# Sums of weight halves interleaved with joins, range sums on ScalarE, and four more units by seven, in a hybrid decoder step

## The chip, the cores and the metric

The kernel runs on one core of a Trainium2 chip. Five engines matter: TensorE (PE, with its weight loads shown as PEld), VectorE (DVE), ScalarE (ACT), GpSimd (POOL) and SyncE (SP), which issues most of the weight transfers. Each engine works through its own list of instructions in order; one waits for another by semaphores. The metric is the device time of one execution in microseconds (us); lower is better.

## The reference

One layer of a decoder, for 256 prompt tokens and 8 sample tokens (T = 264 columns together), model width 2048:

```python
def swiglu(x, wg, wu, wd):
    return (jax.nn.silu(x @ wg) * (x @ wu)) @ wd

h = h + 0.5 * swiglu(rmsnorm(h, norm_ffn1[l]), ffn1_gate[l], ffn1_up[l], ffn1_down[l])
mix, C_f, n_f, m_f, buf = mixing_block(rmsnorm(h, norm_mix[l]), w_in[l], ...)
h = h + mix
h = h + 0.5 * swiglu(rmsnorm(h, norm_ffn2[l]), ffn2_gate[l], ffn2_up[l], ffn2_down[l])
```

The inner width of both feed-forward networks (FFNs) is 5504, that is 43 blocks of 128. The mixing block, a gated linear memory beside a short convolution, takes part in the change only with its output projection. Everything is in float32; the weights are read once.

## The kernel before

**Numbers in halves.** A float32 weight is split into two float16 parts: ScalarE casts the high part (`high`, L257) and VectorE subtracts it from the weight and writes the low part (`low`, L265). Activations are split in the same way. A regular product needs three float16 matmuls for each block of 128 rows: high by high, high by low, low by high (`three`, L397 to L399), each on 264 columns.

**Units.** An FFN is computed in two halves of its 43 blocks (0 to 21, then 22 to 42). For each block there is a gate product and an up product over 16 blocks of rows; this text calls them one unit. After the units of a half come its 16 down products. A regular unit is two products of 48 matmuls.

**By seven.** Some units, and some pairs of down products (20 in the two FFNs, and two pairs of output products in the mixing block), are made together by `product_pair` (L460). It does the high-by-high terms as they are (L486), for two products on 264 columns. The two correction terms are made for two outputs, two neighbouring blocks of rows and two halves of the tokens at once, a product of 2x2 by 2x2 block matrices, by a scheme that needs seven block products instead of eight, each on 132 columns (L469, L470). For this it needs

- sums of the weights' halves: `weight_sums` makes four tiles `s` out of each weight tile in three VectorE steps, L372, L375 and L376, each of which reads the result of the one before;
- sums of token halves of the activations (`token_sums`, L458), once for a group of eight blocks;
- a `join` of the results: ScalarE copies one part out of PSUM (L523), then `rest` runs on VectorE: L526, L527, L530, L531 and L532, and a reduction (L533) that adds up the magnitudes in the last 16 columns of both products, for a verdict on the ranges at the end (`twins`, read by `judge_early`).

A weight tile has up to 16 blocks of 128 by 128. A unit by seven uses two such tiles, each with the first or second eight row blocks of both gate and up; a regular unit uses one tile for the gate and one for up.

**Banks.** PSUM has eight banks, handed out by `bank()`. A regular product takes one, a unit by seven three: `one`, `other` and `more`.

**The order of work** is written by hand. `product` and `product_pair` first call `fetch` until about three weight tiles are on their way (`AHEAD`, `room`): it starts the transfer from the sync queue, issues the cast on ScalarE and keeps the VectorE part of the tile in `held`. `release`, called in the middle of a product and at its end, issues that part: `low`, and for tiles by seven the three steps of `weight_sums` straight behind it. `tick` counts half products in `seq`; `at(delta, fn)` puts a function on an agenda, and the tick that reaches its time runs it. In this way the join of a unit by seven is issued on VectorE in the first tile of the next unit (`at(1.5, rest)`), its SiLU half a product later on ScalarE (`at(2, gate)`), and its product and split later still. Since each engine keeps its order, a step issued late stands behind everything issued earlier on that engine.

**Where units by seven stand.** `GU_SEVEN` lists the blocks, spread evenly over a stretch by `spread(b0, b1, n)`: n of the blocks from b0 to b1 - 1. Before, in the first FFN 9, 11, 12, 14, 16, 17, 19 and 20 in the first half; in the second FFN 5, 7, 8, 10, 11, 13, 14, 16, 17, 19 and 20; in both second halves 24, 25, 27, 28, 30, 31, 33, 34, 36, 37, 39, 40 and 41.

The functions in question, with the line numbers of the profile:

Of the kernel before, what the change touches and what calls it, by code (L numbers as in the profile page):

```python
# [8 lines left out]
F32 = mybir.dt.float32  # L9
# [3 lines left out]
AF = mybir.ActivationFunctionType  # L13
ALU = mybir.AluOpType

D = 2048
KB = D // 128
SEQ = 256
NS = 8
T = SEQ + NS  # L20
DFF = 5504
NFB = DFF // 128
# [15 lines left out]
SEEN = 16  # L38
# [13 lines left out]
def spread(b0, b1, n):  # L52
    return [b0 + i for i in range(b1 - b0) if (i + 1) * n // (b1 - b0) > i * n // (b1 - b0)]


GU_SEVEN = {
    "1": spread(8, 21, 8) + spread(23, NFB - 1, 13), "2": spread(4, 21, 11) + spread(23, NFB - 1, 13),
}
DOWN_SEVEN = {
    ("1", 0): (1, 2, 3, 5, 6, 7), ("1", 1): (1, 2, 4, 5),  # L60
# [5 lines left out]
TH = T // 2  # L66
# [114 lines left out]
def step(ctx: ExitStack, tc: tile.TileContext, a: dict, shared, bad=None):  # L181
    nc = tc.nc
# [14 lines left out]
    tmp = ctx.enter_context(tc.tile_pool(name="tmp", bufs=2))  # L197
# [73 lines left out]
    def fetch():  # L271
# [46 lines left out]
        if not lag[0]:  # L318
            release()
# [14 lines left out]
    def take(key):  # L334
        got, hi, lo, n, _ = ready.pop(0)
        assert got == key, (got, key)
        return hi, lo, n

    def release():
        for lows, tile_, parts in held:  # L340
            for x in lows:
                low(*x)
            ready.append(tile_)
            if tile_[0][1] in ("gu", "dd"):
                sums.append(weight_sums(parts, tile_[3]))
        held.clear()

# [18 lines left out]
    def weight_sums(w, n):  # L366

        m = n // 2
        s = spool[0].tile([128, 4, WK // 2, 2, 128], PART, tag="s", name="s", bufs=3)[:, :, :m]
        a_, b_, d_ = (w[:, i : i + 2 * m - 1 : 2] for i in (0, 1, n + 1))  # L370
        bc = w[:, 1 : 2 * n - 1].rearrange("p (g k) h m -> p g k h m", g=2)[:, :, 0 : 2 * m - 1 : 2]
        nc.vector.tensor_tensor(  # L372
            s[:, 0:2], bc, d_.unsqueeze(1).to_broadcast([128, 2, m, 2, 128]), op=ALU.add
        )
        nc.vector.tensor_tensor(s[:, 2], s[:, 1], b_, op=ALU.add)  # L375
        nc.vector.tensor_tensor(s[:, 3], s[:, 2], a_, op=ALU.add)  # L376
        return s


    seq, agenda = [0], {}  # L380

    def at(delta, fn, *args):
        agenda.setdefault(int(seq[0]) + delta, []).append((fn, args))

    def tick(step=None):
        if step is None:
            seq[0] = int(seq[0]) + 1
        else:
            seq[0] += step
        for fn, args in agenda.pop(seq[0], []):  # L390
            fn(*args)

    def bank():
        return psum.tile([128, 512], F32, tag="ps", name="ps", bufs=8)
# [65 lines left out]
    def product_pair(key, x, forms, order):  # L460


        one, other, more = bank(), bank(), bank()
        left, right = slice(0, TH), slice(TH, T)
        spare = slice(T, T + TH)
        count, k0 = len(order), 0

        def correct(ps, w, x, first, last):
            nc.tensor.matmul(ps, w[0], x[:, 1], start=first, stop=False)  # L469
            nc.tensor.matmul(ps, w[1], x[:, 0], start=False, stop=last)  # L470

        while k0 < count:
            while room() or not ready:
                fetch()
            hi, lo, n = take(key)
            if room():
                fetch()
            if k0 in (0, WK):
                tick()
            s = sums.pop(0)  # L480
            (hi0, lo0), (hi1, lo1) = ((hi[:, r:], lo[:, r:]) for r in (0, n))
            xs = [x[order[k0 + i]] for i in range(n)]
            last = k0 + n == count
            for ps, hi, lo in ((one, hi0, lo0), (other, hi1, lo1)):
                for i in range(n):
                    nc.tensor.matmul(  # L486
                        ps[:, :T], hi[:, i], xs[i][:, 0], start=(k0 + i == 0), stop=False
                    )
                if n % 2:
                    correct(ps[:, :T], (hi[:, n - 1], lo[:, n - 1]), xs[n - 1], False, False)  # L490
            release()
            if last or k0 == 0:
                tick(0.5)
            for f in range(7):
                for i in range(n // 2):
                    first = k0 + i == 0
                    end = last and i == n // 2 - 1 and f in (2, 5, 6)
                    e, o = 2 * i, 2 * i + 1
                    t = forms[k0 // 2 + i]
                    a_, b_, c_ = (hi0[:, e], lo0[:, e]), (hi0[:, o], lo0[:, o]), (hi1[:, e], lo1[:, e])  # L500
                    w = (a_, b_, c_, *((s[:, f, i, 0], s[:, f, i, 1]) for f in (1, 0, 2, 3)))[f]
                    ps, rhs, own = (
                        (one[:, left], xs[e][:, :, left], False),
                        (one[:, spare], xs[o][:, :, left], False),
                        (other[:, left], t[:, 3], False),
                        (more[:, TH : 2 * TH], t[:, 0], True),
                        (more[:, 2 * TH : 3 * TH], t[:, 1], False),
                        (more[:, left], t[:, 2], False),
                        (one[:, right], xs[e][:, :, right], False),
                    )[f]  # L510
                    correct(ps, w, rhs, first and own, end)
            k0 += n
        return one, other, more

    def join(banks):


        one, other, more = banks
        y = spool[0].tile([128, 4, TH], F32, tag="y4", name="y4", bufs=2)
        u = t264("ta")[:, :TH]  # L520
        p = more[:, : 3 * TH].rearrange("p (n t) -> p n t", n=3)
        z = y[:, 0:4].rearrange("p (g s) t -> p g (s t)", g=2)
        nc.scalar.copy(y[:, 0], one[:, T : T + TH])  # L523

        def rest():
            nc.vector.tensor_tensor(u, y[:, 0], p[:, 0], op=ALU.subtract)  # L526
            nc.vector.tensor_tensor(  # L527
                y[:, 1:3], p[:, 1:3], u.unsqueeze(1).to_broadcast([128, 2, TH]), op=ALU.add
            )
            nc.vector.tensor_tensor(y[:, 3], p[:, 1], y[:, 2], op=ALU.add)  # L530
            nc.vector.tensor_tensor(z[:, 0], one[:, :T], z[:, 0], op=ALU.add)  # L531
            nc.vector.tensor_tensor(z[:, 1], other[:, :T], z[:, 1], op=ALU.subtract)  # L532
            nc.vector.tensor_reduce(  # L533
                twins[:, :, next(twin)], y[:, 1:4:2, TH - SEEN :],
                axis=mybir.AxisListType.X, op=ALU.add, apply_absolute_value=True,
            )

        return z, rest

# [112 lines left out]
    if half_size:  # L652
# [3 lines left out]
        twins = const.tile([128, 2, PAIRS], F32, name="twins")  # L656
        twin = iter(range(PAIRS))
# [547 lines left out]
        return ps, 128.0 * (len(verdicts) + n) - 0.5  # L1205

    if half_size:
        at(2 * NFB + 2 * KB - 2, judge_early)
    ffn("2", n2, done, end=end)
    cols = spans[-1]  # L1210
    scaled(0, 4, cols, nc.sync)
# [751 lines left out]
```

## Time and profile before

| what | us |
|---|---|
| median of three runs | 1785.66 (1784.39 to 1786.18) |
| profiled execution | 1784.75, its span 1783.0 |
| TensorE busy in the span | 1769.2 |
| VectorE busy | 1628.6 |
| ScalarE busy | 881.4 |
| GpSimd busy | 180.1 |

The span runs from the first to the last instruction of the program; what lies around it (1.75 us here) is in the time, not in the rows. The rows of a profile give an instruction's line, engine, operation, what it writes and reads by the program's own names, the shape, how often it occurs, and how long it takes; the idle time of the engine ahead of it stands in brackets or in the last column, with what ended it. TensorE's matmuls are pipelined: a row's duration is longer than the distance to the next row's start, and the distance is what a matmul takes out of the time. The granted clock of TensorE was 0.998 over the span.

### The profile page before, as it was taken

What the parts mean: (1) busy time and instruction counts of PE and PEld (TensorE: products, weight loads), DVE (VectorE), ACT (ScalarE), POOL (GpSimd) and SP (SyncE); (2) the same over time, 40 slices, a digit from 0 to 9 for tenths busy, and PEclk for the clock granted to TensorE, in tenths of its full rate; (3) what the DMA queues carried; (4) which work ended last, traced back from release to release, by engine and by line L of the source; (5) the groups of instructions that cost most, each with busy time, mean ns of one, the idle gap of its engine ahead of it and who ended that gap; (6) DMA issues with size and microseconds to landing.
All of it is one profiled execution on the core that took longest, in us unless ns stands there. A gap on an engine that the chain in (4) does not pass through costs nothing.

```text
span 1783.0 us, 45308 instructions
## 1 busy us (share of the span) xinstructions
PE 1769.2 (99%) x19802; PEld 1599.4 (90%) x19802; DVE 1628.6 (91%) x2278; ACT 881.4 (49%) x1256; POOL 180.1 (10%) x200
## 2 busy tenths in 40 slices
PE   9999999999999999999999999999999999999997
PEld 8899999999999998888888888899999999999996
DVE  8999989999999998888888798999989999999896
ACT  7644444344444435567566644544444444443443
POOL 0000000000000341212121044000000000000142
PEclk9999999999999999999999999999999999999999
DMA  9656565675655656987787646565655766564653
GB/s 325 220 194 212 180 206 197 205 250 195 213 191 180 203 168 199 305 298 265 281 282 242 222 170 243 184 236 181 216 170 178 236 231 222 184 216 161 202 190 112
DMA packets 102494, 381.51 MB, mean 214 GB/s; under 512 B 10988, under 2 KB 20812, under 8 KB 93328
## 3 DMA queue, kind: packets, MB, share of 16 engines
q1 hardware_dynamic: 93088, 350.52, 58.5%
q0 software_dynamic: 8256, 27.57, 4.5%
q8 instruction: 157, 2.57, 0.6%
q10 hardware_dynamic: 944, 0.45, 0.1%
q14 instruction: 49, 0.40, 0.1%
HBM read 366.72 MB, written 11.78 MB: 212 GB/s over the span
## 4 chain that ended last, share of the span: by engine, by line
PE 96%; DVE 3%; issue 0%; DMA 0%; ACT 0%; DVEq 0%; SPq 0%; ACTq 0%
PE ps L397 18%; PE ps L399 18%; PE ps L398 18%; PE ps L486 14%; PE ps L469 13%; PE ps L470 13%; PE ps L633 1%; DVE w L265 1%; DVE s L372 0%; PE ps L779 0%; PE ps L1596 0%; PE ps L1539 0%; PE ps L1494 0%; DVE s L375 0%; DVE s L376 0%
## 5 line engine op out<-in xcount | busy, mean ns | idle before, releaser
L265 DVE SCALAR_TENSOR_TENSOR w<-wraw,w 128x2048 f16<-128x2048 f32 (+5 forms) x426 | 761.7, 1804 | 56.7 <-ACT w L257 56.0
L257 ACT ACTIVATE w<-wraw 128x2048 f16<-128x2048 f32 (+5 forms) x426 | 633.3, 1503 | 141.6 <-PE ps L470 49.7
L398 PEld LDWEIGHTS <-w 128*128 128x128 f16 x2890 | 282.8, 98 | 42.6
L397 PEld LDWEIGHTS <-w 128*128 128x128 f16 x2890 | 283.0, 98 | 41.2 <-issue 0.4
L399 PEld LDWEIGHTS <-w 128*128 128x128 f16 x2890 | 282.8, 98 | 41.4 <-DVE w L265 0.2
L397 PE MATMUL ps<-r,w 128*128 128x264 f16 x992 | 273.8, 276 | 0.0
L398 PE MATMUL ps<-r,w 128*128 128x264 f16 x992 | 273.8, 276 | 0.0
L399 PE MATMUL ps<-r,w 128*128 128x264 f16 x992 | 273.8, 276 | 0.0
L486 PEld LDWEIGHTS <-w 128*128 128x128 f16 x2368 | 226.9, 98 | 31.2
L397 PE MATMUL ps<-xm,w 128*128 128x264 f16 x896 | 247.3, 276 | 0.0
L399 PE MATMUL ps<-xm,w 128*128 128x264 f16 x896 | 247.3, 276 | 0.0
L398 PE MATMUL ps<-xm,w 128*128 128x264 f16 x896 | 247.3, 276 | 0.0
L470 PEld LDWEIGHTS <-s 128*128 128x128 f16 x2352 | 228.3, 97 | 0.0
L469 PEld LDWEIGHTS <-s 128*128 128x128 f16 x2352 | 226.8, 96 | 1.2 <-DVE y L530 1.2
L372 DVE TENSOR_TENSOR s<-w 128x2048 f16<-128x2048 f16 (+2 forms) x154 | 184.3, 1196 | 9.9 <-DVE w L265 0.5
L486 PE MATMUL ps<-r,w 128*128 128x264 f16 x1440 | 176.7, 276 | 0.0
L470 PEld LDWEIGHTS <-w 128*128 128x128 f16 x1780 | 173.6, 98 | 2.5
L469 PEld LDWEIGHTS <-w 128*128 128x128 f16 x1780 | 173.4, 97 | 2.5
L397 PE MATMUL ps<-a,w 128*128 128x264 f16 (+2 forms) x554 | 144.3, 268 | 0.0
L398 PE MATMUL ps<-a,w 128*128 128x264 f16 (+2 forms) x554 | 144.3, 268 | 0.0
L399 PE MATMUL ps<-a,w 128*128 128x264 f16 (+2 forms) x554 | 144.3, 268 | 0.0
L469 PE MATMUL ps<-f,s 128*128 128x132 f16 x1080 | 133.7, 220 | 0.8 <-DVE y L530 0.8
(305 smaller groups left out, 2832.5 us busy)
## 6 DMA issues: line engine op xcount, KB each, us to landing
wraw<-in_w2gu SPq DMA_DIRECT2D x86, 1024.0 KB, 5.1
wraw<-in_w1gu SPq DMA_DIRECT2D x74, 1024.0 KB, 5.2
wraw<-in_win SPq DMA_DIRECT2D x112, 512.0 KB, 5.2
wraw<-in_w1d SPq DMA_DIRECT2D x20, 1024.0 KB, 5.0
wraw<-in_w2d SPq DMA_DIRECT2D x20, 1024.0 KB, 5.0
wraw<-in_wout SPq DMA_DIRECT2D x24, 512.0 KB, 4.6
wraw<-in_w1d SPq DMA_DIRECT2D x16, 704.0 KB, 4.0
wraw<-in_w2d SPq DMA_DIRECT2D x16, 704.0 KB, 4.1
```

Of the source, the lines that this page charges most:

```text
L257: nc.scalar.activation(dst, src, AF.Copy, scale=scale)
L265: nc.vector.scalar_tensor_tensor(dst, src, scale, hi, op0=ALU.mult, op1=ALU.subtract)
L372: nc.vector.tensor_tensor(s[:, 0:2], bc, d_.unsqueeze(1).to_broadcast([128, 2, m, 2, 128]), op=ALU.add)
L397: nc.tensor.matmul(ps, wh, xk[:, 0, :], start=first, stop=False)
L398: nc.tensor.matmul(ps, wh, xk[:, 1, :], start=False, stop=False)
L399: nc.tensor.matmul(ps, wl, xk[:, 0, :], start=False, stop=last)
L469: nc.tensor.matmul(ps, w[0], x[:, 1], start=first, stop=False)
L470: nc.tensor.matmul(ps, w[1], x[:, 0], start=False, stop=last)
L486: nc.tensor.matmul(ps[:, :T], hi[:, i], xs[i][:, 0], start=(k0 + i == 0), stop=False)
L633: nc.tensor.matmul(ps[j0 + j], w[:, nk * j + k, :], x[k0 + k][:, part, :], start=(k0 + k + n == 0), stop=(k0 + k == KB - 1 and n == 2),)
```

## The change

There are three parts.

*Order of the sums.* `weight_sums` no longer issues its three steps. It puts them on a list, `chain`, and `drain(n)` issues the first n of the list. `drain` is called by `release` ahead of new sums, at the end of each `tick`, in `product_pair` just before a tile's sums are used, and between the steps of `rest`, one at a time.

*The joins.* The last two steps of `rest` change places (the one on `other` now comes first). The reduction on VectorE is gone; in its place `seen` runs on ScalarE, at the next half or whole tick: two ACTIVATE instructions with an accumulated output, one for each of the two products. `judge_early`, which reads these sums, is issued half a product later.

*The blocks.* One more unit by seven in each half of each FFN: 71 pairs in all instead of 67. By `spread`, the first FFN has 9, 10, 12, 13, 15, 16, 18, 19 and 20 in its first half; the second 5, 6, 8, 9, 11, 12, 13, 15, 16, 18, 19 and 20; both second halves 24, 25, 27, 28, 29, 31, 32, 33, 35, 36, 37, 39, 40 and 41.

```diff
 GU_SEVEN = {
-    "1": spread(8, 21, 8) + spread(23, NFB - 1, 13), "2": spread(4, 21, 11) + spread(23, NFB - 1, 13),
+    "1": spread(8, 21, 9) + spread(23, NFB - 1, 14), "2": spread(4, 21, 12) + spread(23, NFB - 1, 14),
 }
...
+    chain = []
+
+    def drain(n=3):
+
+        for step in chain[:n]:
+            step()
+        del chain[:n]
+
     def release():
...
             if tile_[0][1] in ("gu", "dd"):
+                drain()
                 sums.append(weight_sums(parts, tile_[3]))
...
-        nc.vector.tensor_tensor(
-            s[:, 0:2], bc, d_.unsqueeze(1).to_broadcast([128, 2, m, 2, 128]), op=ALU.add
-        )
-        nc.vector.tensor_tensor(s[:, 2], s[:, 1], b_, op=ALU.add)
-        nc.vector.tensor_tensor(s[:, 3], s[:, 2], a_, op=ALU.add)
+        add = nc.vector.tensor_tensor
+        d2 = d_.unsqueeze(1).to_broadcast([128, 2, m, 2, 128])
+        chain.extend((
+            lambda: add(s[:, 0:2], bc, d2, op=ALU.add),
+            lambda: add(s[:, 2], s[:, 1], b_, op=ALU.add),
+            lambda: add(s[:, 3], s[:, 2], a_, op=ALU.add),
+        ))
...
         for fn, args in agenda.pop(seq[0], []):
             fn(*args)
+        drain()
...
                 tick()
+            drain()
             s = sums.pop(0)
...
             nc.vector.tensor_tensor(u, y[:, 0], p[:, 0], op=ALU.subtract)
+            drain(1)
             nc.vector.tensor_tensor(
                 y[:, 1:3], p[:, 1:3], u.unsqueeze(1).to_broadcast([128, 2, TH]), op=ALU.add
             )
+            drain(1)
             nc.vector.tensor_tensor(y[:, 3], p[:, 1], y[:, 2], op=ALU.add)
+            drain(1)
+            at(1 if seq[0] % 1 else 0.5, seen, next(twin))
+            nc.vector.tensor_tensor(z[:, 1], other[:, :T], z[:, 1], op=ALU.subtract)
             nc.vector.tensor_tensor(z[:, 0], one[:, :T], z[:, 0], op=ALU.add)
-            nc.vector.tensor_tensor(z[:, 1], other[:, :T], z[:, 1], op=ALU.subtract)
-            nc.vector.tensor_reduce(
-                twins[:, :, next(twin)], y[:, 1:4:2, TH - SEEN :],
-                axis=mybir.AxisListType.X, op=ALU.add, apply_absolute_value=True,
-            )
+
+        def seen(n):
+            for g in range(2):
+                nc.scalar.activation(
+                    tmp.tile([128, SEEN], F32, tag="seen", name="seen", bufs=2),
+                    y[:, 1 + 2 * g, TH - SEEN :], AF.Abs, accum_out=twins[:, g, n : n + 1],
+                )
...
-        at(2 * NFB + 2 * KB - 2, judge_early)
+        at(2 * NFB + 2 * KB - 1.5, judge_early)
```

## The prediction

> **What bounds the kernel now.** I read the profile page first, then the busy time by stretch, then the order of time on VectorE and TensorE where two stretches end.
>
> ```profile
> span 1783.0 us, 45308 instructions
> ...
> PE 1769.2 (99%) x19802; PEld 1599.4 (90%) x19802; DVE 1628.6 (91%) x2278; ACT 881.4 (49%) x1256; POOL 180.1 (10%) x200
> ```
>
> TensorE is busy 99% of the span, VectorE 91%, ScalarE 49%. Two engines stand near the limit, so the stretches matter more than the page. The next rows are stretches (length, then busy time and count of TensorE, weight load, VectorE, ScalarE and GpSimd, then clock and DMA): one regular gate/up unit, one unit by seven, a group of two by seven and one regular, then the gate/up part of the second half of the first FFN, and the first down projection.
>
> ```profile
> 1607.01:1617.81 10.80, 10.80 (x99) 9.40 (x97) 10.53 (x15) 5.28 (x8) 0.00 (x0) 1.00 0.62 197
> 1617.81:1627.85 10.04, 10.04 (x146) 9.57 (x144) 9.77 (x12) 4.64 (x6) 0.00 (x0) 1.00 0.53 183
> 1576.13:1607.01 30.88, 30.88 (x387) 28.54 (x385) 30.16 (x38) 14.33 (x18) 0.00 (x0) 1.00 0.63 213
> ...
> 372.90:558.18 185.28, 184.70 (x2354) 171.40 (x2352) 178.60 (x222) 82.72 (x103) 0.00 (x0) 1.00 0.57 194
> 253.40:351.31 97.91, 97.91 (x1325) 92.08 (x1323) 93.14 (x109) 39.35 (x34) 0.00 (x0) 1.00 0.60 200
> ```
>
> The reader is to see three things. TensorE has no idle time in a unit: 10.80 us regular, 10.04 us by seven, at a granted clock of 1.00. So TensorE sets the end, and what a unit by seven is worth is 10.80 - 10.04 = 0.76 us. VectorE runs beside it at 30.16 of 30.88 us in a group: it is nearly a second bound. And the gate/up stretch has 185.28 us against 184.70 busy, so almost nothing stalls.
>
> Where it does stall is at the third of three units by seven in a row (blocks 39, 40, 41), once in each FFN. The first fence shows the second of the two places on TensorE, the second what that join line (L530) ends for others.
>
> ```profile
> 1641.02 0.22 PE L470 MATMUL ps<-f,w 128*128 128x132 f16 x1
> 1641.49 0.23 PE L469 MATMUL ps<-f,s 128*128 128x132 f16 x1 [0.26 <-DVE y L530]
> ```
>
> ```profile
>   PEld L469: 1.2, 2
> ```
>
> These matmuls follow each other every 0.06 us, so the start at 1641.49 instead of 1641.08 is a stall of 0.41 us; the two places together cost 1.2 us. The matmul is the first into the third unit's bank `more`. A unit takes three of eight banks, so the third in a row gets one that the first's join still reads, and L530 is the last reader of that join's `more`. Block 39 ended at 1627.85 (above), so a join is late if L530 ends more than 1641.08 - 1627.85 = 13.2 us after its unit.
>
> **What the change costs, part by part.** (1) Four more units by seven, one in each half of each FFN: on TensorE 4 x 0.76 = 3.04 us less. Weight bytes and their DMA issues stay as they are, two 1 MB loads a unit in both forms.
>
> (2) VectorE. This is the whole of its work for one unit by seven, from block 37's and 38's tiles in order of time:
>
> ```profile
> 1609.35 2.29 DVE L265 SCALAR_TENSOR_TENSOR w<-wraw,w 128x2048 f16<-128x2048 f32 x1
> 1611.67 1.23 DVE L372 TENSOR_TENSOR s<-w 128x2048 f16<-128x2048 f16 x1
> 1612.93 0.69 DVE L375 TENSOR_TENSOR s<-s,w 128x1024 f16<-128x1024 f16 x1
> 1613.66 0.69 DVE L376 TENSOR_TENSOR s<-s,w 128x1024 f16<-128x1024 f16 x1
> 1614.27 0.28 DVE L526 TENSOR_TENSOR ta<-y,ps 128x132 f32<-128x132 f32 x1
> 1614.58 0.43 DVE L527 TENSOR_TENSOR y<-ps,ta 128x264 f32<-128x264 f32 x1
> 1615.05 0.29 DVE L530 TENSOR_TENSOR y<-ps,y 128x132 f32<-128x132 f32 x1
> 1615.26 0.42 DVE L531 TENSOR_TENSOR y<-ps,y 128x264 f32<-128x264 f32 x1
> 1615.60 0.42 DVE L532 TENSOR_TENSOR y<-ps,y 128x264 f32<-128x264 f32 x1
> 1616.06 0.19 DVE L533 TENSOR_REDUCE twins<-y 128x2 f32<-128x32 f32 x1
> 1616.17 2.29 DVE L265 SCALAR_TENSOR_TENSOR w<-wraw,w 128x2048 f16<-128x2048 f32 x1
> 1618.49 1.23 DVE L372 TENSOR_TENSOR s<-w 128x2048 f16<-128x2048 f16 x1
> 1619.75 0.69 DVE L375 TENSOR_TENSOR s<-s,w 128x1024 f16<-128x1024 f16 x1
> 1620.48 0.69 DVE L376 TENSOR_TENSOR s<-s,w 128x1024 f16<-128x1024 f16 x1
> 1621.09 0.43 DVE L265 SCALAR_TENSOR_TENSOR a<-y,a 128x264 f16<-128x264 f32 x1
> 1621.43 0.42 DVE L939 SCALAR_TENSOR_TENSOR y<-y,tb 128x264 f32<-128x264 f32 x1
> 1621.78 0.42 DVE L939 SCALAR_TENSOR_TENSOR tc<-ps,tb 128x264 f32<-128x264 f32 x1
> 1622.12 2.28 DVE L265 SCALAR_TENSOR_TENSOR w<-wraw,w 128x2048 f16<-128x2048 f32 x1
> ```
>
> Read it by starts. First tile with the join: 1609.35 to 1616.17, 6.82 us. Second tile: to 1621.09, 4.92. Split of an activation 0.34, product with the gate 0.35. Together 12.43 us against 10.04 on TensorE, so each unit by seven puts VectorE 2.4 us behind. A regular unit has two weight splits of 2.29 - 0.08 = 2.21, one split of 0.34 and one product of 0.34: 5.10 us against 10.80.
>
> Now the gaps. L372 ends at 1612.90 and L375, which reads its result, starts at 1612.93: 0.03 us idle. L376 ends at 1614.35, but L526, which has nothing of it, starts at 1614.27: 0.08 us overlap. All pairs in the fence fall so: a step that needs the one just before it starts 0.03 to 0.04 us after its end, any other 0.08 before. Putting a foreign step between two linked ones is thus worth 0.115 us. The change does that to six links of the first tile (weight split to sum, sum to sum twice, L526 to L527, L527 to L530, and the last join step to the reduction): 0.69 us. The reduction itself leaves, 0.11 us. In the second tile the product comes between the weight split and the first sum, 0.115 us, while the three sums stay linked. A unit falls to 12.43 - 0.69 - 0.11 - 0.115 = 11.52 us.
>
> [...]
>
> The sums of tokens for a group of eight activations come on top, four steps of 0.70 us, 0.35 us a unit:
>
> ```profile
> L458 DVE TENSOR_TENSOR g<-a 128x1056 f16<-128x1056 f16 x16 | 10.6, 702 | 0.1
> ```
>
> Before, two by seven and one regular: 2 x 12.43 + 5.10 + 3 x 0.35 = 31.0 us of VectorE in 30.88 of TensorE. After, three and one, which is the new pattern of the second halves: 3 x 11.52 + 5.10 + 4 x 0.35 = 41.1 us in 40.92. The balance stays what it was, and a run of three costs a backlog of 3 x 1.48 = 4.4 us where two cost 4.8 and the one run of three cost 7.2.
>
> (3) Late joins. There are now eleven runs of three instead of two. In a steady group block 37, which ended at 1607.01, had its L530 end at 1615.34: 8.3 us later against the limit of 13.2, so 4.9 us in hand. In the changed order that step stands before the last sum instead of behind all three, about 1 us earlier behind its weight split. With the smaller backlog I take no stall at any run of three and both old ones gone: -1.2 us. Bounds: none gone (0), or each of nine new runs late by the mean of the two old ones, 0.6 us (+5.2).
>
> (4) ScalarE gets two range sums for each of 71 pairs. The nearest row is its range sum over a regular product, which takes two instructions:
>
> ```profile
> 1582.02 0.18 ACT L670 ACTIVATE seen<-ps 128x16 f32<-128x16 f32 x1
> 1582.08 0.20 ACT L670 ACTIVATION_READ_ACCUMULATOR seen<-ps 128x1 f32 x1
> 1582.17 1.91 ACT L257 ACTIVATE w<-wraw 128x2048 f16<-128x2048 f32 x1
> ```
>
> That is 0.15 us, so 0.30 us a unit on an engine that works 4.64 of 10.04 us there: nothing, covered by its idle time. It adds a wait, though: ScalarE does not go on to the next weight cast until the join's last step is done. In gate/up units the SiLU in front of it waits for that same join already. In down units the wait is new; VectorE then still has the next weight split and its sums, whose cast was issued ahead of the wait, so it does not run dry. I take 0; the other bound is the fourth rival.
>
> (5) The order of the sums. They now follow up to three join steps (0.20 + 0.35 + 0.21 us by starts), so the first sum comes 0.1 us and the last about 0.5 us later behind its weight split, which the shorter queue ahead of it gives back. The verdict on the range sums, 5.3 us of VectorE near the end, moves by half a product and changes places with one weight split; what follows both has the same sum ahead of it. I take 0, at worst one such split of 1.5 us:
>
> ```profile
> 1749.02 0.24 DVE L731 TENSOR_SCALAR ta<-stat 128x172 f32<-128x172 f32 x1
> ...
> 1754.33 3.01 DVE L265 SCALAR_TENSOR_TENSOR w<-wraw,w 128x1408 f16<-128x1408 f32 x2
> ```
>
> Sum: -3.04 - 1.2 = -4.2 us. The profiled execution took 1784.75 us (its span and 1.75 around it), so 1780.5 by its own time. The three runs' median, 1785.66, lies 0.9 above it, so **1781.5 us** as a median.
>
> **Rivals.**
> - The stalls stay. The two waits of 1.2 us remain because blocks 39 to 41 are the same blocks with the same token sums in front. Then only 3.04 us go: 1782.6, or -0.17%. For it: those 2.8 us of token sums fall into that run still. Against: by then VectorE has saved 14 x 0.91 us and paid 11.52 - 5.10 for the added unit, so it comes there some 6 us less loaded.
> - New waits for banks. Each of nine new runs of three pays 0.6 us: 1785.66 - 3.04 + 5.2 = 1787.8. For it: the only run of three in the trace is the only place that stalls. It decides when L530 ends more than 13.2 us after its unit; against it stands the 8.3.
> - Interleaving gains nothing on VectorE, the slower case. Place: second halves, three by seven to one regular. A unit then costs 12.32 us, a group 3 x 12.32 + 6.50 = 43.5 in 40.92, 2.5 us short; 19 blocks are 4.75 groups, 12 us, of which the 4.9 in hand take a part: 7 us in each FFN, 1785.66 - 3.04 + 14 = 1797. It decides once a unit by seven costs VectorE more than (40.92 - 6.50) / 3 = 11.5 us over a whole half plus what is in hand, about 11.8. Against it: the gaps above.
> - ScalarE holds the casts back in the down projections. If each of the 20 down units loses a cast and a range sum (1.91 + 0.30 us) on VectorE, the six of the first take 13.3 us, of which 97.91 - 93.14 = 4.8 idle and 6 x 0.8 of saved links cover 9.6; 3.7 is left, times 20 / 6 for all of them 12 us: 1793.5. It decides only if VectorE has less than 2.2 us of work between the join's end and the next split that needs that cast; the fence shows a split and three sums there, 4.9 us.
>
> **How the numbers follow.** Forecast 0.50, stalls stay 0.24, new waits 0.10, no gain from interleaving 0.06, ScalarE 0.06, others 0.04. A measurement of this kernel can tell about 0.2%, 3.6 us, from no change, and the forecast of 4.2 lies just beyond: of its 0.50 I give 0.40 to faster and 0.10 to same; of the first rival 0.03 and 0.21. With the second mostly same, and the third and fourth slower: faster 0.45, same 0.42, slower 0.13. The range goes from 1780.2 (the forecast less the runs' spread) to 1787.0, which takes in the first rival and part of the second; the likeliest alone would be 1780.5 to 1782.5.
>
> **What would show it.** TensorE busy down by 3 us and no wait of a weight load on a join; stretches of three and one of 40.9 us with VectorE busy for some 40; start to start between L372's and L375's counterparts near 1.14 us in the tile with a join and still 1.26 in the other; ScalarE up by about 20 us. The forecast is wrong if any wait of TensorE on VectorE over 1 us in sum appears in the gate/up stretches or the down projections, or if the links do not shorten.

## The result, and the profile after

The changed kernel takes 1780.43 us in the median of 11 runs (1780.1 to 1781.63), the kernel before, run beside it, 1785.07 (1784.3 to 1786.18): a ratio of 0.9975, with a 95% interval of 0.9967 to 0.9984. That is 4.64 us less. The profiled execution took 1780.68 us with a span of 1779.0, 4.0 us less than before.

The profile page of the changed kernel: busy times, and the first line of the chain of work that ended last (each engine's share of the span).

```profile
PE 1765.9 (99%) x19994; PEld 1600.2 (90%) x19994; DVE 1629.8 (92%) x2255; ACT 906.3 (51%) x1528; POOL 169.2 (10%) x200
...
PE 99%; DMA 0%; DVE 0%; SPq 0%; ACT 0%; issue 0%; DVEq 0%; ACTq 0%
```

The same line of the chain in the kernel before:

```profile
PE 96%; DVE 3%; issue 0%; DMA 0%; ACT 0%; DVEq 0%; SPq 0%; ACTq 0%
```

TensorE is busy 3.3 us less, and VectorE's 3% are gone from the chain: in the feed-forward networks its work no longer holds TensorE back, apart from two matmuls that start 0.08 us late (below). VectorE is as busy as before, with four more units by seven. ScalarE has 24.9 us more.

What TensorE waited for (line, releaser and its line: us in total, times, longest). First the one line of the kernel before that has no counterpart after; then all lines after, which stood before too, the one on a cast (`part`) with 0.5 instead of 0.9 us:

```profile
PE ps L469 <- DVE y L530: 0.8, 2, 0.6
```

```profile
PE ps L1224 <- DVE ta L1218: 2.3, 1, 2.3
PE idle L228 <- DVE ones L218: 1.1, 1, 1.1
PE ps L653 <- ACT part L257: 0.9, 3, 0.5
PE ps L799 <- DVE sq L1186: 0.2, 1, 0.2
```

The wait for the last reader of `more` (L530 before, L545 after) is gone; what remains stands outside the feed-forward networks. (New lines: the sums are L384 to L386, the steps of the join L539, L541, L545, L548, L549, ScalarE's copy L536, the corrections L481 and L482.)

The end of the second FFN's second half, after: the first, third and last of four groups of three units by seven and a regular one, and one unit by seven (length, then busy time and count of TensorE, weight load, VectorE, ScalarE and GpSimd, clock, DMA).

```profile
1480.83:1521.75 40.92, 40.92 (x532) 38.11 (x529) 39.25 (x50) 20.00 (x35) 0.00 (x0) 1.00 0.62 206
...
1562.67:1603.59 40.92, 40.92 (x532) 38.11 (x529) 40.07 (x50) 20.12 (x38) 0.00 (x0) 1.00 0.64 209
1603.59:1644.60 41.01, 41.01 (x531) 38.10 (x529) 40.50 (x53) 18.09 (x35) 0.00 (x0) 1.00 0.51 170
1614.39:1624.43 10.04, 10.04 (x147) 9.57 (x144) 9.80 (x11) 5.25 (x11) 0.00 (x0) 1.00 0.48 147
```

The groups take 40.92 us, exactly 3 x 10.04 + 10.80. VectorE's busy time in the groups shown rises from 39.25 to 40.50, since it has less idle time, and the last group is 0.09 us too long. The place on TensorE:

```profile
1637.59 0.22 PE L482 MATMUL ps<-f,w 128*128 128x132 f16 x1
1637.73 0.23 PE L481 MATMUL ps<-f,s 128*128 128x132 f16 x1
```

0.06 us after 1637.59 would be 1637.65, so this start is 0.08 us late (in the first FFN as much). The unit whose bank it wants, block 39, ended at 1624.43 (fence above), so the bank was wanted 13.2 us after it. The join that frees it is the second L545 in VectorE's rows; the first is the same join of the run before (block 35, which ended at 1562.67 + 10.80 + 10.04 = 1583.51):

```profile
1594.11 0.28 DVE L545 TENSOR_TENSOR y<-ps,y 128x132 f32<-128x132 f32 x1
...
1630.30 1.32 DVE L470 TENSOR_TENSOR g<-a 128x1056 f16<-128x1056 f16 x2
1631.54 0.70 DVE L470 TENSOR_TENSOR g<-g,a 128x1056 f16<-128x1056 f16 x1
...
1637.38 0.29 DVE L545 TENSOR_TENSOR y<-ps,y 128x132 f32<-128x132 f32 x1
```

Block 35's bank is free 1594.39 - 1583.51 = 10.9 us after its unit, block 39's 1637.67 - 1624.43 = 13.24. The changed kernel stands exactly at the limit of 13.2 us, not well inside it. VectorE does not lose this time bit by bit: the first joins of the four runs of three end 8.5, 11.1, 10.9 and 13.2 us after their units, and the two steps up are where the sums of tokens stand (L470, four steps, 1630.30 to the next weight split at 1632.90, 2.6 us). A group without them gains 0.2 us.

VectorE's order of time, the interleaved tile first, then a join that has no sums to mix with:

```profile
1567.39 2.29 DVE L265 SCALAR_TENSOR_TENSOR w<-wraw,w 128x2048 f16<-128x2048 f32 x1
1569.59 0.28 DVE L539 TENSOR_TENSOR ta<-y,ps 128x132 f32<-128x132 f32 x1
1569.79 1.22 DVE L384 TENSOR_TENSOR s<-w 128x2048 f16<-128x2048 f16 x1
1570.93 0.42 DVE L541 TENSOR_TENSOR y<-ps,ta 128x264 f32<-128x264 f32 x1
1571.27 0.68 DVE L385 TENSOR_TENSOR s<-s,w 128x1024 f16<-128x1024 f16 x1
1571.87 0.29 DVE L545 TENSOR_TENSOR y<-ps,y 128x132 f32<-128x132 f32 x1
1572.07 0.68 DVE L386 TENSOR_TENSOR s<-s,w 128x1024 f16<-128x1024 f16 x1
...
1573.36 2.28 DVE L265 SCALAR_TENSOR_TENSOR w<-wraw,w 128x2048 f16<-128x2048 f32 x1
...
1600.79 0.29 DVE L539 TENSOR_TENSOR ta<-y,ps 128x132 f32<-128x132 f32 x1
1601.11 0.43 DVE L541 TENSOR_TENSOR y<-ps,ta 128x264 f32<-128x264 f32 x1
1601.58 0.29 DVE L545 TENSOR_TENSOR y<-ps,y 128x132 f32<-128x132 f32 x1
1601.91 0.43 DVE L548 TENSOR_TENSOR y<-ps,y 128x264 f32<-128x264 f32 x1
```

In the first tile every step starts 0.08 us before its predecessor ends; the tile takes 1573.36 - 1567.39 = 5.97 us, where 6.02 was predicted. In the second piece the steps stand 0.03 to 0.04 us apart, as before the change, and the new order has linked L548 to L545 too. How often each occurs is in VectorE's groups (busy, mean ns of one, idle time just before them):

```profile
L385 DVE TENSOR_TENSOR s<-s,w 128x1024 f16<-128x1024 f16 (+1 forms) x162 | 111.2, 686 | 4.5
...
L541 DVE TENSOR_TENSOR y<-ps,ta 128x264 f32<-128x264 f32 x71 | 30.5, 429 | 1.4
```

The same groups before:

```profile
L375 DVE TENSOR_TENSOR s<-s,w 128x1024 f16<-128x1024 f16 (+2 forms) x154 | 106.7, 693 | 5.3
...
L527 DVE TENSOR_TENSOR y<-ps,ta 128x264 f32<-128x264 f32 x67 | 28.9, 432 | 2.3
```

Before, each of 67 joins had the gap: 2.3 / 67 = 0.034 us. After, 1.4 us are 41 such gaps among 71 joins. So only 30 joins are interleaved; in the other 41 the tile that the join follows belongs to a regular product, or has no sums waiting. In order of time, the join at 1569.59 is of a run's third unit (block 33, which ended at 1562.67), the one at 1600.79 of a second (block 36). Tiles are split ahead of their use: while block 37 is computed, VectorE splits those of the regular block 38, which need no sums. In each of the eight runs of three in the second halves the second unit's join is linked in this way, at the half's end also the last unit's (block 41).

### The profile page after: what moved, and what is told of

Same layout as the page of the kernel before. It is cut to its first block, busy times and chain, and to the rows that moved or that the text cites. A ratio compares the mean times of both kernels' runs of the same rounds, so it can differ in the third digit from the quotient of the medians.

```text
span 1779.0 us, 46011 instructions
## 1 busy us (share of the span) xinstructions
PE 1765.9 (99%) x19994; PEld 1600.2 (90%) x19994; DVE 1629.8 (92%) x2255; ACT 906.3 (51%) x1528; POOL 169.2 (10%) x200
## 4 chain that ended last, share of the span: by engine, by line
PE 99%; DMA 0%; DVE 0%; SPq 0%; ACT 0%; issue 0%; DVEq 0%; ACTq 0%
PE ps L409 17%; PE ps L410 17%; PE ps L411 17%; PE ps L499 16%; PE ps L481 14%; PE ps L482 14%; PE ps L653 1%; PE ps L799 0%; PE ps L1616 0%; DMA raw<-in_w1gu 0%; PE ps L1559 0%; PE ps L1514 0%; DVE h L1167 0%; PE ps L1538 0%; PE ps L1600 0%; PE ps L1537 0%
## 5 line engine op out<-in xcount | busy, mean ns | idle before, releaser
L482 PEld LDWEIGHTS <-s 128*128 128x128 f16 x2480 | 240.7, 97 | 0.0
L481 PEld LDWEIGHTS <-s 128*128 128x128 f16 x2480 | 238.9, 96 | 0.2
L409 PE MATMUL ps<-r,w 128*128 128x264 f16 x864 | 238.5, 276 | 0.0
L410 PE MATMUL ps<-r,w 128*128 128x264 f16 x864 | 238.5, 276 | 0.0
L411 PE MATMUL ps<-r,w 128*128 128x264 f16 x864 | 238.5, 276 | 0.0
L384 DVE TENSOR_TENSOR s<-w 128x2048 f16<-128x2048 f16 (+1 forms) x162 | 191.9, 1185 | 6.1 <-PE ps L482 1.0
L499 PE MATMUL ps<-r,w 128*128 128x264 f16 x1568 | 192.5, 276 | 0.0
L482 PEld LDWEIGHTS <-w 128*128 128x128 f16 x1876 | 183.0, 98 | 2.6
L481 PEld LDWEIGHTS <-w 128*128 128x128 f16 x1876 | 182.8, 97 | 2.6
L481 PE MATMUL ps<-f,s 128*128 128x132 f16 x1176 | 145.6, 220 | 0.0
L482 PE MATMUL ps<-f,s 128*128 128x132 f16 x1176 | 145.4, 219 | 0.0
L409 PE MATMUL ps<-a,w 128*128 128x264 f16 (+2 forms) x554 | 144.3, 268 | 0.0
L410 PE MATMUL ps<-a,w 128*128 128x264 f16 (+2 forms) x554 | 144.3, 268 | 0.0
```

Of the source, the lines that this page charges most:

```text
L384: lambda: add(s[:, 0:2], bc, d2, op=ALU.add),
L409: nc.tensor.matmul(ps, wh, xk[:, 0, :], start=first, stop=False)
L410: nc.tensor.matmul(ps, wh, xk[:, 1, :], start=False, stop=False)
L411: nc.tensor.matmul(ps, wl, xk[:, 0, :], start=False, stop=last)
L499: nc.tensor.matmul(ps[:, :T], hi[:, i], xs[i][:, 0], start=(k0 + i == 0), stop=False)
```

## Experiments

Each ran beside the kernel before on the same chip; the ratios are to that kernel, with 95% intervals. Its medians there were 1784.77 to 1784.83 us, 1785.07 beside the changed kernel, so differences of a few tenths between experiments mean nothing.

**The blocks alone.** The order of VectorE stays as it was.

```diff
@@ GU_SEVEN, kernel before @@
-    "1": spread(8, 21, 8) + spread(23, NFB - 1, 13), "2": spread(4, 21, 11) + spread(23, NFB - 1, 13),
+    "1": spread(8, 21, 9) + spread(23, NFB - 1, 14), "2": spread(4, 21, 12) + spread(23, NFB - 1, 14),
```

> Kernel before with the new blocks alone: 14 units by seven in each second half, 9 and 12 in the first halves; sums and reduction as before. Theory A (VectorE's backlog makes joins late once a unit by seven costs it 12.4 us): a second half of 19 blocks is 14 x 12.43 + 5 x 5.10 + 19 x 0.35 = 206 us of VectorE in 194.6 of TensorE, 12 us short, where before it was 198.8 in 195.3, 3.5 short with 0.6 of stall. So about 9 us of stall in each second half and 0 to 3 in the second FFN's first half: 1785.1 - 3.0 + 19 = about 1801, at least 1793; the trace shows TensorE waiting for joins in the runs of three. Rival B (the units alone carry the gain, the order is immaterial): 1785.1 - 3.0 = 1782 or, if the old stalls go by the new places, 1781.

Measured: 1821.86 us, 1.0209 [1.0195, 1.0223]. The units alone make the kernel 37 us slower: theory A's way, but 21 us more than its 1801. The largest wait of TensorE, then the last of its nine stalls, on VectorE and on TensorE:

```profile
PE ps L469 <- DVE y L530: 32.0, 9, 6.0
```

```profile
1671.28 2.29 DVE L265 SCALAR_TENSOR_TENSOR w<-wraw,w 128x2048 f16<-128x2048 f32 x1
1673.67 1.23 DVE L372 TENSOR_TENSOR s<-w 128x2048 f16<-128x2048 f16 x1
...
1676.27 0.29 DVE L526 TENSOR_TENSOR ta<-y,ps 128x132 f32<-128x132 f32 x1
...
1677.06 0.29 DVE L530 TENSOR_TENSOR y<-ps,y 128x132 f32<-128x132 f32 x1
```

```profile
1671.18 0.22 PE L470 MATMUL ps<-f,w 128*128 128x132 f16 x1
1677.41 0.29 PE L469 MATMUL ps<-f,s 128*128 128x132 f16 x1 [6.01 <-DVE y L530]
```

TensorE wants the bank at 1671.24, and the join that has to free it is still behind a weight split and three sums on VectorE. The account: 3.04 us less for the units, 0.8 less for the two old waits, 32.0 for the nine new ones, together 28.2; the span grew by 37.1. The remaining 8.9 us are in matmuls after the stalls: behind five of them the granted clock is 0.50 for 3.03, 3.58, 4.08, 3.29 and 3.83 us (last section), 17.8 us in all, of which half is lost. (Counted by the starts of matmuls a stall is some 0.15 us longer than by these waits, so the account is good to about 1 us.)

**The order alone.** The changed kernel with the old blocks.

```diff
@@ GU_SEVEN @@
-    "1": spread(8, 21, 9) + spread(23, NFB - 1, 14), "2": spread(4, 21, 12) + spread(23, NFB - 1, 14),
+    "1": spread(8, 21, 8) + spread(23, NFB - 1, 13), "2": spread(4, 21, 11) + spread(23, NFB - 1, 13),
```

> Changed kernel with the old blocks (13, 8, 11): interleaved sums and ScalarE's range sums without more units. Theory A: only the two stalls of 1.2 us go, since TensorE waits for nothing else: 1785.1 - 1.2 = 1783.9, TensorE's waits on joins gone. Rival B: the order does nothing for the stalls, 1785.1. If VectorE were itself on the path all along, more would come off: under 1783.

Measured: 1784.02 us, 0.9998 [0.9989, 1.0007], a span 1.3 us shorter, and no wait of TensorE on a join. By the medians alone this can't be told from no change; in the trace the two old stalls are gone. The order's worth is that it carries four more units.

**The sums in one piece.** The changed kernel, but the three sums are issued as soon as their tile is split, ahead of the join. The move to ScalarE stays.

```diff
@@ weight_sums @@
             lambda: add(s[:, 3], s[:, 2], a_, op=ALU.add),
         ))
+        drain()
```

> Changed kernel, new blocks and ScalarE's range sums, but the three sums are issued straight behind their weight split, so nothing is interleaved. Theory A (a linked step costs 0.115 us more): a unit costs VectorE about 12.3 us instead of 11.5 to 12.0, so second halves are some 10 us short instead of 3.5 before: 6 to 7 us of stall in each, 1785.1 - 3.0 + 14 = about 1796, at least 1787. Rival C (a link costs nothing, the room came from the reduction that moved to ScalarE): as the changed kernel, 1780 to 1782.

Measured: 1822.34 us, 1.0212 [1.0198, 1.0226], the same as the blocks alone. So the move of the range sums does not carry the gain, and the order of sums and joins is worth 42 us, far more than the 16 that theory A gave. That the two kernels take the same is in part chance: TensorE waits 27.6 us for joins here and 32.0 there, but runs 26.4 us at half the clock here and 17.8 there. TensorE's largest wait, and the waits of VectorE and ScalarE in the gate/up part of the first FFN's second half (372 to 556 us):

```profile
PE ps L482 <- DVE y L546: 27.6, 9, 5.1
```

```profile
ACT y L537 <- DVE a L265: 13.3, 3, 4.5
...
DVE w L265 <- ACT w L257: 7.6, 8, 1.9
```

VectorE, which is too slow here, idles 7.6 us in that stretch for a cast of ScalarE. One such place, first on VectorE, then on ScalarE:

```profile
436.75 0.43 DVE L265 SCALAR_TENSOR_TENSOR a<-y,a 128x264 f16<-128x264 f32 x1
437.09 0.43 DVE L960 SCALAR_TENSOR_TENSOR y<-y,tb 128x264 f32<-128x264 f32 x1
439.39 2.29 DVE L265 SCALAR_TENSOR_TENSOR w<-wraw,w 128x2048 f16<-128x2048 f32 x1 [1.88 <-ACT w L257]
```

```profile
437.28 0.27 ACT L537 COPY y<-ps 128x132 f32<-128x132 f32 x1 [4.45 <-DVE a L265]
437.45 1.91 ACT L257 ACTIVATE w<-wraw 128x2048 f16<-128x2048 f32 x1
```

ScalarE's copy writes one of two `y4` tiles, and must wait until VectorE has split the activation out of the tile (436.75). The cast stands behind the copy in ScalarE's queue, and VectorE's next weight split stands behind the cast. A late VectorE thus makes itself later by 1.88 us. Whether this is a real part of the cost is tested further down.

**The reduction on VectorE.** The changed kernel without the move to ScalarE.

```diff
@@ rest @@
-            at(1 if seq[0] % 1 else 0.5, seen, next(twin))
             nc.vector.tensor_tensor(z[:, 1], other[:, :T], z[:, 1], op=ALU.subtract)
             nc.vector.tensor_tensor(z[:, 0], one[:, :T], z[:, 0], op=ALU.add)
+            nc.vector.tensor_reduce(
+                twins[:, :, next(twin)], y[:, 1:4:2, TH - SEEN :],
+                axis=mybir.AxisListType.X, op=ALU.add, apply_absolute_value=True,
+            )
```

> Changed kernel with the range sums back on VectorE, as one reduction at the end of the join, behind the step that it reads. Theory A: 0.11 + 0.115 us a unit more on VectorE, 14 x 0.22 = 3.1 us in a second half whose reserve at the last run of three is used up in the changed kernel: 2 to 3 us of stall in each, 1780.4 + 5 = 1785, between 1782.5 and 1787. Rival (the reduction is immaterial, interleaving made all the room): 1780.4. Rival C (the reduction made all the room): as slow as the run without interleaving or slower, 1790 and more.

Measured: 1782.25 us, 0.9983 [0.9974, 0.9992]. Two stalls of 0.6 us are back at the ends of the second halves, where the changed kernel stands at the limit. The move is worth 1.8 us by the medians and 1.7 by the spans (1780.7 against 1779.0), less than expected; the intervals of the two kernels overlap, and it is the stalls that show the difference.

**The whole join first.** Nothing is interleaved: all steps of the join, then the sums.

```diff
@@ rest, three times @@
-            drain(1)
```

> Changed kernel, but the whole join stands ahead of the newest tile's three sums, with nothing between its steps: five linked steps a tile with a join, one fewer than in the run with the sums at once (1822 us) and five more than in the changed kernel (1780). Its step that frees the bank (fourth quarter of the join) then ends 1.0 us after the weight split in front, where it is 2.6 in the changed kernel and 3.7 with the sums at once. Theory A, as predicted (what counts is VectorE's time for a unit): nearly as slow as with the sums at once, 1810 to 1822. Theory P (what counts is the place of the join in VectorE's queue, since only the bank makes TensorE wait): 1780 to 1786, waits of TensorE on joins under 3 us.

Measured: 1785.02 us, 1.0002 [0.9993, 1.0011]. This tells two readings of the 42 us apart. Sums first 1822.34, join first 1785.02: that is 37 us. Most of it is the join's place in VectorE's queue, since few links go with it. Counted in VectorE's rows, the steps of sums and joins that start 0.03 to 0.04 us behind the step just before them are 622 with the sums first, 552 with the join first and 402 in the changed kernel. The first 70 links, 8 us of VectorE's time at 0.115 each, are part of the 37 us. The other 150, 17 us of its time, go with the last 4.6 us, from join first 1785.02 to interleaved 1780.43. TensorE waits 2.7 us for joins here, at the last runs of three, and 1.1 us for weight splits. VectorE's rows in this kernel, and its wait for casts in the same stretch as above:

```profile
1570.70 2.29 DVE L265 SCALAR_TENSOR_TENSOR w<-wraw,w 128x2048 f16<-128x2048 f32 x1
...
1573.69 0.29 DVE L543 TENSOR_TENSOR y<-ps,y 128x132 f32<-128x132 f32 x1
```

```profile
DVE w L265 <- ACT w L257: 2.7, 2, 1.9
```

The last reader of `more` starts 2.99 us after its weight split here, 1571.87 - 1567.39 = 4.48 us in the changed kernel and 1677.06 - 1671.28 = 5.78 us with the blocks alone. VectorE's idle time for casts falls from 7.6 to 2.7 us, so part of the 37 us may go this way (tested further down). (In the changed kernel it is 4.6 us in this stretch, without a stall.)

**Sums at other places too.** The changed kernel with one sum issued behind each function of the agenda.

```diff
@@ tick @@
         for fn, args in agenda.pop(seq[0], []):
             fn(*args)
+            drain(1)
```

> Changed kernel with one waiting sum also issued behind each function of a tick's agenda, which parts two more links in the second tile of a unit, up to 0.23 us a unit of VectorE. Theory A and P alike: TensorE has 0.2 us of such stalls left, so nothing is to be had: 1780.4, between 1779.8 and 1781.2. If VectorE's time were itself on the path, 14 units would give 2 to 3 us a half: under 1778.

Measured: 1780.62 us, 0.9977 [0.9967, 0.9987]. The edit brings nothing, but it also saves next to nothing: 35 second sums no longer wait for the first, while 15 first sums and 15 last join steps now wait for the step before them, 396 short gaps in place of 402. What many more saved links would bring it does not show; TensorE, which waits on no join any more, has 0.16 us to gain.

**One unit more in each second half.** Does the balance carry a fifteenth?

```diff
@@ GU_SEVEN @@
-    "1": spread(8, 21, 9) + spread(23, NFB - 1, 14), "2": spread(4, 21, 12) + spread(23, NFB - 1, 14),
+    "1": spread(8, 21, 9) + spread(23, NFB - 1, 15), "2": spread(4, 21, 12) + spread(23, NFB - 1, 15),
```

> Changed kernel with 15 instead of 14 units by seven in both second halves: runs of three and of four. TensorE alone would give 2 x 0.76 us: 1778.9 (rival: there is room left). Theory A and P: a run of four costs a backlog of 4 x 1.48 = 5.9 us and more against some 5 in hand, and a group of five is 4 x 11.52 + 5.10 + 1.75 = 52.9 us of VectorE in 50.96: stalls of 1 to 4 us at each of three runs of four in each FFN, 1785 to 1805, about 1793.

Measured: 1794.65 us, 1.0052 [1.0038, 1.0065]. Runs of four stall: six waits of TensorE on a join, 10.8 us in all, the longest 4.0.

**Fifteen, with the join ahead of the sums.** The last kernel's fifteen units again; since the join's place counted for so much, its first three steps stay together, and the sums come behind them.

```diff
@@ rest @@
             nc.vector.tensor_tensor(u, y[:, 0], p[:, 0], op=ALU.subtract)
-            drain(1)
...
-            drain(1)
             nc.vector.tensor_tensor(y[:, 3], p[:, 1], y[:, 2], op=ALU.add)
             drain(1)
...
             nc.vector.tensor_tensor(z[:, 1], other[:, :T], z[:, 1], op=ALU.subtract)
+            drain(1)
@@ tick @@
             fn(*args)
+            drain(1)
```

> The 15 units of the run beside it with the join ahead of the sums (its first three steps together, then sums between its last two) and the waiting sums parted by the agenda as well. Theory P: the bank is free 1.6 us sooner, so stalls are much smaller than in the run beside it: 1779 to 1785. Theory A (time for a unit alone): two links more in one tile and two fewer in the other, so as slow as the run beside it.

Measured: 1797.01 us, 1.0067 [1.0054, 1.0081], with 14.5 us of waits on the join. Theory P's expectation failed, and the links did not cancel as the expectation took it: 445 steps wait for the one just before them, 396 in the last kernel, and VectorE is busy 1646.3 us instead of 1641.6. A reading that fits, not tested by itself: an earlier place helps while VectorE has the time to catch up between the runs; once it lacks the time itself, the place cannot make it, and the links that this order gives back cost more than it gains.

**The copy behind the cast.** The kernel with the sums in one piece, but ScalarE's copy is issued later.

```diff
@@ join @@
-        nc.scalar.copy(y[:, 0], one[:, T : T + TH])
+        at(1, nc.scalar.copy, y[:, 0], one[:, T : T + TH])
```

> The run with the sums at once (1822 us), but ScalarE's copy that begins a join is issued one tick later, behind the next weight cast. There a third unit's copy waited for VectorE's split of the first unit's activations (two buffers for the join's results), the cast stood behind the copy, and VectorE sat idle 1.88 us for it at each run of three but the first. Theory Q (this idle time is a good part of what the order costs): some 5 us of stall less in each second half, with the slow clock behind it 12 to 17 us in all: 1805 to 1812. Theory P alone (only VectorE's own work and the join's place count): 1820 to 1823.

Measured: 1805.79 us, 1.0119 [1.0103, 1.0134], that is 16.5 us less than with the copy in its old place. VectorE's idle time for casts in the stretch:

```profile
DVE w L265 <- ACT w L257: 0.6, 3, 0.2
```

7.6 us became 0.6, and over the whole run TensorE's waits on joins fell from 27.6 to 17.8 us, its time at half the clock from 26.4 to 10.0. So the casts behind the copy, with the slow clock that their stalls bring, were 16.5 of the 42 us. The remaining 25 lie between the late joins themselves and the links; these were not divided further.

**Fifteen in five runs of three.** The same count of units, no run of four.

```diff
@@ GU_SEVEN @@
-    "1": spread(8, 21, 9) + spread(23, NFB - 1, 14), "2": spread(4, 21, 12) + spread(23, NFB - 1, 14),
+    "1": spread(8, 21, 9) + spread(22, NFB - 1, 15), "2": spread(4, 21, 12) + spread(22, NFB - 1, 15),
```

> Changed kernel with 15 units by seven in each second half, set as five runs of three with one regular unit ahead of each (22, 26, 30, 34, 38) instead of runs of three and four. TensorE alone: 1780.4 - 1.5 = 1778.9. By theory P stalls are what the first join of a run is late over 13.2 us; VectorE has 6.8 us more to do in the half, against 3 us of idle time at its start and a last run that is at 13.3 already, so 4 us of stall in each FFN: 1787, between 1781 and 1792, well under the 1794.7 of 15 units with runs of four. If the length of a run alone decided, no stalls: 1779.

Measured: 1786.92 us, 1.0012 [1.0003, 1.0021], with four stalls (0.77, 1.94, 1.05 and 1.95 us). Better than runs of four by 7.7 us, but the fifteenth unit costs time in either arrangement.

**The same with the copy later.**

```diff
@@ join @@
-        nc.scalar.copy(y[:, 0], one[:, T : T + TH])
+        at(1, nc.scalar.copy, y[:, 0], one[:, T : T + TH])
```

> The run beside it (five runs of three) with ScalarE's copy one tick later, behind the next weight cast. Theory Q: VectorE loses its waits for casts at these runs, 1 to 3 us in a half, and the stalls shrink by as much: 1780 to 1786, under the run beside it. Theory P alone: the same as the run beside it.

Measured: 1784.39 us, 0.9998 [0.9989, 1.0007]: 2.5 us better, still 4 us behind the changed kernel.

**The changed kernel with the copy later.** The same edit, in the kernel as changed, with its fourteen units in the second halves.

```diff
@@ join @@
-        nc.scalar.copy(y[:, 0], one[:, T : T + TH])
+        at(1, nc.scalar.copy, y[:, 0], one[:, T : T + TH])
```

> The changed kernel as it is, but ScalarE's copy of a join is issued half a product to a whole one later, so that the cast behind it does not stand behind the wait for the split of the unit before. In the changed kernel TensorE waits on a join nowhere; what is left are starts 0.08 us late at the third unit of two runs of three, 0.16 us in all. If only TensorE's waits count, this can bring no more than that: 1780.2 to 1780.5 us, ratio to the kernel before 0.9975, no wait of TensorE on a join. If the late copy makes the join itself later at the ends of the runs of three (the first join step waits for the copy), stalls come back: each join 0.5 us later there would cost 0.5 us in two to four places, 1781.5 to 1782.5.

Measured: 1780.61 us, 0.9976 [0.9967, 0.9985], no wait of TensorE on a join. The copy costs the changed kernel nothing. No version here beats it.

## Why the prediction was right, step by step

The time was predicted as 1781.5 us and came out at 1780.43; by the profiled executions, 4.2 us less were predicted and 4.0 measured. The forecast's case is the one that happened. Of the 1.1 us between the two times 0.6 are the kernel before, which took 1785.07 us beside the changed one where the forecast started from 1785.66. The working holds less well than the sum, and that the old stalls went without new ones is in part luck.

- **The worth of a unit (step 1): right.** A unit by seven takes 10.04 us and a regular one 10.80 in both kernels; the groups of 40.92 us show it.
- **The price of a link (step 2): right, its count wrong.** The gap of 0.03 and the overlap of 0.08 us came as read, and the interleaved tile took 5.97 us against 6.02. But the step took six links from every unit, and only 30 of 71 joins found sums to stand between. "A unit falls to 11.52 us" fits two units of a run of three; the second keeps its linked join, as the rows above show.
- **Late joins (step 3): right in the outcome, wrong in the margin.** The step took 4.9 us in hand from block 37, the second unit of a run of two in the kernel before. The join that counts is the first of a run of three: 10.9 us after its unit at the last run but one, 13.2 at the last, so nothing is in hand there. The step spread the sums of tokens as 0.35 us a unit; they come in one piece of 2.6 us, right ahead of that join, as the first rival said. It is luck that the limit just held: with the reduction back on VectorE, some 0.22 us a unit by the rows, both stalls are back. And the earlier place, noted as "about 1 us" and not priced, 1.3 us by the rows, is not a side effect: sums first and join first differ by 37 us.
- **ScalarE (step 4): mis-sized, without effect.** Two range sums take 0.40 us by starts, where 0.30 was taken: 24.9 us on the page instead of some 20, with eight regular products' range sums fewer. The row, from ScalarE's order of time in the changed kernel:

```profile
1573.86 0.20 ACT L553 ACTIVATE seen<-y 128x16 f32<-128x16 f32 x1
...
1574.26 0.16 ACT L690 ACTIVATE seen<-ps 128x16 f32<-128x16 f32 x1
```

- **Order of the sums, verdict and down projections (steps 4 and 5): right.** In the first down projection, 253.03 to 350.95 in the changed kernel, TensorE is busy 97.92 of 97.92 us, as long as before (97.91).
- **The third rival was priced too low.** "Interleaving gains nothing" was given 1797; the kernel that has its order takes 1822.34. The term that failed is "7 us in each FFN": it counted VectorE's missing time, once. The trace has 27.6 us of waits on joins in place of 14, and 26.4 us at half the clock, which is 13.2 lost. The term lacked three things that the runs showed: the join stands behind the sums of a further tile, and TensorE stalls at nine of the eleven runs of three; ScalarE's copy waits for VectorE and holds the next cast (16.5 us with what followed); and the clock halves after seven of the nine stalls (0.50 from 517.12 on). The first rival, that the stalls stay, was right in its mechanism, the sums of tokens ahead of that join, and fell by a hair: 0.16 us late in all where 1.2 were. The second and the fourth show no trace.

With the sums ahead of the joins, the same four units lose more than ten times the 3 us that they are worth.

## What to carry to other kernels

In a queue that runs in order, ask first which of its instructions another engine waits for, and put that ahead of work that nobody waits for yet; here this moved most of 37 us and the shorter gaps 5. Give the lateness of that instruction as a number against the moment it is wanted, at the worst run and not at a steady one. Look there for work that comes in one piece, which an average over units hides: 2.6 us of token sums took the last run to the limit. On an engine that is nearly a second bound (VectorE, 40.07 of 40.92 us in a group) the order of its queue decides whether a backlog becomes stalls, and what waits behind the late engine can hold it back in turn (1.88 us of VectorE's idle time at one place with the sums in one piece).

## What was not expected of the hardware

Some stalls of TensorE are followed by slow matmuls: with the sums in one piece those on 132 columns then start every 0.11 us instead of every 0.06. TensorE in the kernel with the blocks alone, right behind its last stall (length, busy, counts, clock, DMA):

```profile
1677.41:1681.40 3.99, 3.99 (x35) 3.90 (x36) 3.92 (x7) 2.39 (x3) 0.00 (x0) 0.52 0.00 0
```

After 6.01 us without work the granted clock is 0.52 over the next 3.99 us; from 1681.40 on it is 1.00 again. Five of the nine stalls in that kernel were 3.8 us or longer, and the slow stretches stand behind these five; each costs 1.8 us (8.9 / 5) beside its own length.

Among stalls of about 2 us the length does not tell. With the blocks alone one of 1.99 us, from 515.82 to 517.81, leaves the clock at 1.00; with the sums in one piece one of 1.92 us, from 514.18 to 516.10, is followed by half the clock, and not at once but from 517.12 on. With the sums in one piece the slow stretches before the program's end start at 472.74, 517.12, 561.49, 1329.49, 1585.49, 1629.86 and 1677.65 us, whole multiples of 3.413 us apart, and last one or two such steps. With the blocks alone the last one ends at 1677.41 + 3.83 = 1681.24, 341 such steps behind 517.29. These are the steps around the two stalls, first with the blocks alone, then with the sums in one piece:

```profile
513.88:517.29 3.41, 1.94 (x30) 1.71 (x27) 3.20 (x6) 0.00 (x0) 0.00 (x0) 1.00 0.52 166
517.29:520.70 3.41, 2.89 (x42) 2.76 (x43) 3.34 (x6) 2.39 (x3) 0.00 (x0) 1.00 0.35 142
```

```profile
513.70:517.12 3.42, 1.50 (x27) 1.33 (x25) 3.28 (x8) 0.18 (x1) 0.00 (x0) 1.00 0.76 292
517.12:520.53 3.41, 3.41 (x27) 2.83 (x25) 3.04 (x3) 3.41 (x9) 0.00 (x0) 0.50 0.11 13
```

The first stall is parted by the steps, 1.47 and 0.52 us of it in one each; the second lies in one step whole. In the feed-forward networks with the sums in one piece seven steps at full speed have 1.92 to 3.03 us of idle time in them, and each is followed by half the clock; no other has more than 1.77, and none of these is. That holds for this trace alone: in the run with fifteen units and the join ahead of the sums a step with 2.00 us idle kept the clock.
